# Moving weight sums of a block-form product from VectorE to accumulating transfers, with the late splits moved to the middle of a pair and two more chunks in block form

## The chip, the cores and the metric

The kernel runs on one core of a Trainium2 chip. The metric is the device time of one execution in microseconds. An engine is named as the profile names it: PE is TensorE's matmuls, PEld its weight loads, DVE VectorE, ACT ScalarE, POOL GpSimd, SP SyncE, which here only issues transfers.

## The reference, cut to what matters

One layer over 512 latent tokens (a grid of 8 x 64) of 1024 channels, with 256 context tokens and 16 heads of 64 channels:

```python
h  = rmsnorm(x) * (1 + sc) + sh;  hc = rmsnorm(ctx) * (1 + sc_c) + sh_c
b_gate, c_gate, x_in, z_a, q, k, v, z_b, g_a, g_b = split(h @ w_in)      # 10 parts of 1024 columns
q, k = rope(q), rope(k)                                                 # 2-D rotary
k_c, v_c = split(hc @ w_in[:, K_OFF:V_END])
attn = softmax([q.k over an 8 x 16 window + rpb, q.k_c]) @ [v, v_c]
y_a = (silu(z_a) * b_gate * conv3(c_gate * x_in)) @ w_out_conv
y_b = (silu(z_b) * attn) @ w_out_attn
y   = (sigmoid(g_a) * y_a + sigmoid(g_b) * y_b) @ w_o
out = x + gt * rmsnorm(y)
```

Everything is float32.

## The kernel before

**Products.** A float32 operand is split into a high part H (an ACT cast) and a low part L (a DVE subtraction); the helper `split` does both (L67 the cast, L70 or L73 the subtraction), and a product is three matmuls, H·H, H·L and L·H.

**Chunks.** The weights of the input projection come in chunks of 1 MB, 256 columns each, as two `raw` tiles of 512 KB (4 of 8 row blocks each), loaded by SP (L89). The pool has three `raw` buffers, so the second raw tile of chunk n+1 lies in the buffer of chunk n's first one. In the program's names a chunk is qk (queries and keys of one head pair), v (values), zb (attention's gate), cx and bz (the two chunks of a convolution part) or g (merge gates). `order` lists the chunks in the order in which they are used, and `plan` says which are worked on beside which head pair's attention. A plain chunk is split as it stands and multiplied in 2 x 24 matmuls of 512 columns (L164 to L166). For a chunk that `paired` names, the product is taken in a block form with seven half-size products: `pair` runs 7 x 12 matmuls of 256 columns (L289) into three PSUM banks a, b and e. Its operands of weights are B11, B21, B22 (parts of the raw tiles) and T1 to T4 (sums of parts). `Chunk.first` adds b11+b12 (L102, T1), b11+b22 (L105, T2), b12+b22 (L109, T3) and b21+b11 (L110, T4), in place in the raw tiles, and splits B11, T1, B21 and T2. `Chunk.second` splits T3, T4 and B22 when the pair begins. The qk chunks (`keep`) also need B12, so that their b12+b22 is added in `second`. Twenty chunks are paired before: qk3, 4 and 6, zb0 to zb2, cx5 to 7, bz5 to 7, g0 to g7.

**Attention's slots.** The attention part is 8 head pairs of 8 slots. A slot takes steps of the filling generators (`step(items)`, that is pairs and units of the chunks of this row of `plan`), then the score block two ahead (L717 to L726, softmax on L733 to L747), after every second block the transposes of the weights and their split into TH and TL (L754, then `split`), and once in four blocks the weighted values (`gather`, L773). At a slot's end the functions in `behind` run: there the next chunk's `first` is done. `later` holds functions that are due some steps on: of a paired qk the queries' split and copies (`queries`), and the keys' (`rest`). `rope` rotates one projection with two DVE products and two accumulating transfers on POOL's queue (L626).

**Order.** The instructions of an engine run in the order that the framework's scheduler gives them, apart from those that are held in the order of the program (`keep_in_program_order`). Within a queue each waits for those ahead of it.

The host lays out the weights before the launch; the part b11 of a raw tile is 4 strips of 128 columns of a row of 256.

Of the kernel before, what the change touches and what calls it, by code (L numbers as in the profile page):

```python
# [27 lines left out]
def layer(ctx: ExitStack, tc, xp, ctxt, ctxT, cc, wmod, small, wfirst, win, wout, wo, rel, tab, out):  # L28
# [35 lines left out]
    def split(H, L, src, scale=None, pinned=False):  # L64

        if scale is None:
            cast = nc.scalar.copy(H, src)  # L67
            if pinned:
                tc.keep_in_program_order(cast)
            nc.vector.tensor_sub(L, src, H.bitcast(F32))  # L70
        else:
            nc.scalar.mul(H, src, scale)
# [10 lines left out]
    class Chunk:  # L83
# [7 lines left out]
        def split(self):  # L91
            t = [wtile([P, 4, 2, 256]) for _ in range(2)]
            for x, raw in zip(t, self.raws):
                split(x[:, :, 0], x[:, :, 1], raw)
            k = range(KT)
            return tuple([t[i // 4][:, i % 4, y] for i in k] for y in range(2)) + ([t[i // 4][:, i % 4] for i in k],)

        def first(self, keep=False):
            (b11, b12), (b21, b22) = self.b = [(r[:, :, :P], r[:, :, P:]) for r in self.raws]
            t, sums = (wtile([P, 2, 2, 4, P]) for _ in range(2))  # L100
            split(t[:, 0, 0], t[:, 0, 1], b11)
            nc.vector.tensor_add(b11, b11, b12)  # L102
            split(sums[:, 0, 0], sums[:, 0, 1], b11)
            split(t[:, 1, 0], t[:, 1, 1], b21)
            nc.vector.tensor_add(b11, b11, b22)  # L105
            split(sums[:, 1, 0], sums[:, 1, 1], b11)
            self.keep = keep
            if not keep:
                nc.vector.tensor_add(b12, b12, b22)  # L109
            nc.vector.tensor_add(b21, b21, b11)  # L110
            self.B = {"B11": t[:, 0], "B21": t[:, 1], "T1": sums[:, 0], "T2": sums[:, 1]}
            return self

        def second(self):
            t, last = (wtile([P, 2, 2, 4, P]) for _ in range(2))
            (_, b12), (b21, b22) = self.b
# [11 lines left out]
    class Chunks:  # L128
# [104 lines left out]
    def paired(n, i):  # L233
        return n == "g" or n == "qk" and i in (3, 4, 6) or n == "zb" and i < 3 or n in ("cx", "bz") and i > 4
# [59 lines left out]
    def pair(c1, c2, w=None):  # L294

        w = w or chunk().B
# [3 lines left out]
        nc.scalar.copy(c1[:, first], a)  # L300
        product(b, A12, w["B21"], True)
# [4 lines left out]
        nc.vector.tensor_add(c1[:, first], c1[:, first], b)  # L306
# [324 lines left out]
    def step(items):  # L631
# [4 lines left out]
        next(items)  # L636
        for f, units in due:
# [20 lines left out]
    def keys_queries(p):  # L658
# [35 lines left out]
        if blocks:  # L694
            later.append((queries, 0))
# [508 lines left out]
```

## Time and profile before

| | before |
|---|---|
| median of 3 runs | 709.12 us (709.09 to 709.35) |
| the profiled execution | 709.01 us, of it span 707.2 |
| instructions of PE, DVE, ACT, POOL | 4196, 1114, 868, 110 |
| chunks in block form | 20 |
| transfers of `raw` from the input weights | 74 of 512 KB, 4.4 us to landing |
| accumulating transfers of the rotations (L626) | 32 of 128 KB, 3.6 us to landing |

Times are microseconds from the span's start unless marked ns. A group's row gives its engine, what it writes and reads with partitions x elements, its count, its busy time and the mean of one instruction. In a timeline "[3.08 <-DMA raw<-in_win]" behind a row says that the engine stood idle 3.08 us before it and that this transfer ended the wait. Matmuls overlap, so what one costs is read from the starts of consecutive ones and not from their durations. In the chain of work that ended last, a row is a stretch of one engine's instructions.

### The profile page before, as it was taken

To read this page: it belongs to the slowest core of one execution; us is meant where nothing else is said; L and a number is where in the kernel's file an instruction comes from. 1 tells how busy PE (TensorE), PEld (TensorE's weight loads), DVE (VectorE), ACT (ScalarE), POOL (GpSimd) and SP (SyncE) were. 2 spreads that over 40 slices of the span, in tenths; PEclk is the share of its full clock that TensorE was granted. 3 is DMA by queue.
4 is the path that set the end of the run, shared out by engine and by line. 5 is a ranking of instruction groups with operands and counts; after the bars stand their busy time and mean duration, and the time that the engine had idled before them with its cause. 6 is when DMAs were issued, how large, how long until landed. Compare 5 with 4: busy or idle time off the path is not lost.

```text
span 707.2 us, 11426 instructions
## 1 busy us (share of the span) xinstructions
PE 695.0 (98%) x4196; PEld 618.0 (87%) x4196; DVE 586.3 (83%) x1114; ACT 436.5 (62%) x868; POOL 66.9 (9%) x110
## 2 busy tenths in 40 slices
PE   7999999999999999999999999999999999999996
PEld 4888888888889989898999999999898899988885
DVE  6979997668599989978898797999799676665996
ACT  6566632656577677775876766778693444442563
POOL 0000002230130310301302203000000000000000
PEclk9999999999999999999999999999999999999998
DMA  8996896564351563542635436313733233560013
GB/s 338 406 354 227 284 339 173 131 164 144 99 105 24 135 176 116 127 138 60 168 106 165 103 125 157 101 61 105 247 117 116 87 120 120 198 250 30 31 59 120
DMA packets 37466, 108.27 MB, mean 153 GB/s; under 512 B 5025, under 2 KB 5281, under 8 KB 37410
## 3 DMA queue, kind: packets, MB, share of 16 engines
q1 hardware_dynamic: 28946, 92.20, 37.8%
q0 software_dynamic: 8320, 15.21, 10.7%
q8 instruction: 33, 0.54, 0.3%
q14 instruction: 23, 0.19, 0.1%
q10 hardware_dynamic: 144, 0.13, 0.1%
HBM read 87.07 MB, written 5.24 MB: 131 GB/s over the span
## 4 chain that ended last, share of the span: by engine, by line
PE 91%; DVE 4%; DMA 2%; ACT 1%; issue 1%; SPq 0%; POOL 0%; DVEq 0%; ACTq 0%
PE ps L289 25%; PE ps L164 11%; PE ps L166 11%; PE ps L165 11%; PE ps L177 6%; PE ps L1008 5%; PE ps L773 4%; PE ps L754 3%; PE ps L182 3%; PE ps L717 3%; PE ps L196 2%; PE ps L424 2%; PE ps L428 2%; PE ps L425 2%; DMA fraw<-in_wfirst 1%; PE ps L726 1%
## 5 line engine op out<-in xcount | busy, mean ns | idle before, releaser
L67 ACT CAST w<-raw 128x512 fp32r<-128x512 f32 (+1 forms) x193 | 137.3, 733 | 95.9 <-PE ps L166 31.3
L70 DVE TENSOR_TENSOR w<-raw,w 128x512 fp32r<-128x512 f32 (+1 forms) x193 | 156.6, 824 | 42.3 <-ACT w L67 40.9
L289 PE MATMUL ps<-S,w 128*128 128x256 f32 x960 | 121.9, 283 | 0.0
L289 PEld LDWEIGHTS ps<-S,w 128*128 128x128 f32 x960 | 118.2, 192 | 0.1
L289 PE MATMUL ps<-h,w 128*128 128x256 f32 x720 | 94.0, 284 | 0.6 <-DVE tc L306 0.5
L289 PEld LDWEIGHTS ps<-h,w 128*128 128x128 f32 x720 | 89.9, 191 | 2.5 <-DVE tc L306 0.7
L164 PE MATMUL ps<-h,w 128*128 128x512 f32 x208 | 81.5, 392 | 0.0
L166 PE MATMUL ps<-h,w 128*128 128x512 f32 x208 | 81.2, 390 | 0.0
L165 PE MATMUL ps<-h,w 128*128 128x512 f32 x208 | 81.0, 390 | 0.0
L626 POOL DMA_DIRECT2D tc<-tb x32 | 28.8, 1175 | 286.7 <-DVE tc L624 197.7
L747 ACT ACTIVATE pt<-pt,z 128x512 f32<-128x512 f32 x64 | 43.0, 724 | 6.0 <-DVE z L745 5.9
L166 PEld LDWEIGHTS ps<-h,w 128*128 128x128 f32 x208 | 39.0, 188 | 8.3
L165 PEld LDWEIGHTS ps<-h,w 128*128 128x128 f32 x208 | 39.1, 188 | 8.0
L164 PEld LDWEIGHTS ps<-h,w 128*128 128x128 f32 x208 | 39.1, 188 | 7.9
L67 ACT CAST TH<-ps 128x512 fp32r<-128x512 f32 x64 | 35.8, 589 | 15.5 <-PE ps L754 15.5
L733 DVE CUSTOM_DVE_ANT_1 ps<-ps,bt 128x512 f32<-128x512 f32 x56 | 38.8, 693 | 6.8 <-PE ps L717 6.5
L70 DVE TENSOR_TENSOR TL<-ps,TH 128x512 fp32r<-128x512 f32 x64 | 42.2, 682 | 1.0 <-ACT TH L67 0.7
L754 PE MATMUL ps<-ident,pt 128*128 128x128 f32 x256 | 33.3, 273 | 0.0
L177 PE MATMUL ps<-w,h 128*128 128x512 f32 x128 | 32.3, 394 | 0.0
L754 PEld LDWEIGHTS ps<-ident,pt 128*128 128x128 f32 x256 | 29.2, 140 | 2.1 <-ACT pt L747 0.2
L740 ACT ACTIVATE pt<-ps,m 128x512 f32<-128x512 f32 x32 | 22.0, 688 | 12.5 <-DVE m L733 11.8
L773 PE MATMUL ps<-TH,V 128*128 128x256 f32 (+1 forms) x96 | 28.5, 319 | 0.2 <-ACT TH L67 0.2
(249 smaller groups left out, 1387.8 us busy)
## 6 DMA issues: line engine op xcount, KB each, us to landing
raw<-in_win SPq DMA_DIRECT2D x74, 512.0 KB, 4.4
wm<-in_wmod SPq DMA_DIRECT2D x34, 512.0 KB, 6.4
raw<-in_wout SPq DMA_DIRECT2D x16, 512.0 KB, 3.6
bt<-in_rel SPq DMA_DIRECT2D x16, 256.0 KB, 2.9
tc<-tb POOLq DMA_DIRECT2D x32, 128.0 KB, 3.6
B<-in_wo SPq DMA_DIRECT2D x8, 512.0 KB, 6.4
fraw<-in_wfirst SPq DMA_DIRECT2D x8, 384.0 KB, 8.6
qd<-qd POOLq DMA_DIRECT2D x24, 128.0 KB, 2.3
```

The source lines that it names most:

```text
L67: cast = nc.scalar.copy(H, src)
L70: nc.vector.tensor_sub(L, src, H.bitcast(F32))
L164: nc.tensor.matmul(ps, lhsT=H[k][:, cs], rhs=mH[k], start=k == 0, stop=False)
L165: nc.tensor.matmul(ps, lhsT=H[k][:, cs], rhs=mL[k], start=False, stop=False)
L166: nc.tensor.matmul(ps, lhsT=L[k][:, cs], rhs=mH[k], start=False, stop=k == KT - 1)
L177: nc.tensor.matmul(ps, lhsT=mH[k][:, ts], rhs=both[k].rearrange("p a c -> p (a c)"), start=k == 0, stop=False, skip_group_check=True,)
L289: nc.tensor.matmul(ps, lhsT=w[:, x, k], rhs=act[y][k], start=start and k + o == 0, stop=k == 3 and o == 2, skip_group_check=True,)
L733: nc.vector.tensor_tensor_reduce(out=s3, in0=s3, in1=bt[:, e::4 - e][:, 0:2], scale=-1.0, scalar=3.0e38, op0=ALU.add, op1=ALU.min, accum_o ...
L747: nc.scalar.mul(x, x, z[:, i:i + 1])
L754: nc.tensor.transpose(tp[:, c], pt[:, c * P:(c + 1) * P], ident)
L773: nc.tensor.matmul(o3[:, dst], lhsT=V[p][:, kt, h], rhs=src(t), start=n == 0 and t is TH, stop=n == len(work) - 1 and t is TL,)
L1008: nc.tensor.matmul(out, lhsT=a(x, k, ts), rhs=w[y][k // 2][:, k % 2, cols], start=start and k + o == 0, stop=k == 3 and o == 2, skip_group ...
```

## The change

1. In paired chunks up to zb3 (`late`: the first 34 of `order`), b12+b22 (not for qk) and b21+b11 become accumulating transfers on POOL's queue, 128 x 512 elements each.
2. In these chunks T3 and T4 are split by a new function `third`, which `pair` calls in the middle, after its first four products; the last three products run in the order B22, T3, T4 instead of T4, T3, B22. The outputs' combinations change order.
3. The rotations of a paired qk run at the slot's end, through `behind`. Its queries' split runs in the middle of the next pair (`midway`).
4. Casts of raw tiles (and of T3, T4 and of paired queries) are held in program order.
5. qk7 and zb3 become paired: 22 chunks in block form.
6. The host lays the paired chunks out so that b11, b12, b21 and b22 are each contiguous in a partition.

```diff
         def split(self):
...
-                split(x[:, :, 0], x[:, :, 1], raw)
+                split(x[:, :, 0], x[:, :, 1], raw, pinned=behind is not None)
...
-        def first(self, keep=False):
-            (b11, b12), (b21, b22) = self.b = [(r[:, :, :P], r[:, :, P:]) for r in self.raws]
+        def first(self, keep=False, late=False):
+            (b11, b12), (b21, b22) = self.b = [
+                [x[:, 2 * u:2 * u + 2].rearrange("p k (x c) -> p (k x) c", c=P) for u in range(2)] for x in self.raws
+            ]
+            self.late = late
             t, sums = (wtile([P, 2, 2, 4, P]) for _ in range(2))
-            split(t[:, 0, 0], t[:, 0, 1], b11)
+            split(t[:, 0, 0], t[:, 0, 1], b11, pinned=behind is not None)
             nc.vector.tensor_add(b11, b11, b12)
+            if late and not keep:
+                nc.gpsimd.dma_start(b12, b22, accum_op=ALU.add)
             split(sums[:, 0, 0], sums[:, 0, 1], b11)
-            split(t[:, 1, 0], t[:, 1, 1], b21)
+            split(t[:, 1, 0], t[:, 1, 1], b21, pinned=behind is not None)
             nc.vector.tensor_add(b11, b11, b22)
+            if late:
+                nc.gpsimd.dma_start(b21, b11, accum_op=ALU.add)
             split(sums[:, 1, 0], sums[:, 1, 1], b11)
             self.keep = keep
-            if not keep:
-                nc.vector.tensor_add(b12, b12, b22)
-            nc.vector.tensor_add(b21, b21, b11)
+            if not late:
+                if not keep:
+                    nc.vector.tensor_add(b12, b12, b22)
+                nc.vector.tensor_add(b21, b21, b11)
...
         def second(self):
...
-            for n, x, b in (("T3", t[:, 0], b12), ("T4", t[:, 1], b21), ("B22", last[:, 0], b22)):
-                split(x[:, 0], x[:, 1], b)
+            if not self.late:
+                self.third()
+            split(last[:, 0, 0], last[:, 0, 1], b22)
+
+        def third(self):
+            t = wtile([P, 2, 2, 4, P])
+            (_, b12), (b21, _) = self.b
+            for n, x, b in (("T3", t[:, 0], b12), ("T4", t[:, 1], b21)):
+                split(x[:, 0], x[:, 1], b, pinned=self.late)
                 self.B[n] = x
...
     def paired(n, i):
-        return n == "g" or n == "qk" and i in (3, 4, 6) or n == "zb" and i < 3 or n in ("cx", "bz") and i > 4
+        return n == "g" or n == "qk" and i in (3, 4, 6, 7) or n == "zb" or n in ("cx", "bz") and i > 4
...
         nc.scalar.copy(c1[:, first], a)
+        while midway:
+            midway.pop(0)()
         product(b, A12, w["B21"], True)
         product(e, blocks_h["X1"], w["T1"], True)
         nc.scalar.copy(c2[:, second], e)
         product(a, blocks_h["S2"], w["T2"], False)
         nc.scalar.copy(c2[:, first], a)
         nc.vector.tensor_add(c1[:, first], c1[:, first], b)
+        if c.late:
+            c.third()
         chunk.more()
         yield
-        product(b, A22, w["T4"], True)
+        if c.late:
+            product(e, blocks_h["S4"], w["B22"], False)
+        else:
+            product(b, A22, w["T4"], True)
         product(a, blocks_h["S3"], w["T3"], False)
         nc.scalar.copy(c1[:, second], a)
-        product(e, blocks_h["S4"], w["B22"], False)
-        for cols, x in ((second, c1[:, second]), (first, e)):
+        if c.late:
+            product(b, A22, w["T4"], True)
+        else:
+            product(e, blocks_h["S4"], w["B22"], False)
+        for cols, x in ((first, e), (second, c1[:, second])):
...
-            rope(q, q)
-            rope(k, k)
+            behind.extend([lambda: rope(q, q), lambda: rope(k, k)])
...
-                split(qd[0][:, dst], qe[0][:, dst], q[:, src], 0.125)
+                split(qd[0][:, dst], qe[0][:, dst], q[:, src], 0.125, pinned=blocks)
...
-            later.append((queries, 0))
+            later.append((lambda: midway.append(queries), 0))
```

Lines move down by 1 to 29 in the changed kernel: L289 becomes L304, L70 stays, L626 becomes L654, L67 becomes L66, L717 becomes L746, L754 L783, L773 L802.

DVE around cx5's `first` (raw_2547 and raw_2548 are cx5's raw tiles, w_2575 holds B11 and B21, w_2576 T1 and T2; TL_2343 is the low part of a slot's transposed weights). Before:

```order
L733 ISA ps_2551,m_2554<-ps_2551,bt_1039 128x512
L733 ISA m_2554 128x1
L70 TENSOR_TENSOR w_2575<-raw_2548,w_2575 128x512
L70 TENSOR_TENSOR TL_2343<-ps_2561,TH_2342 128x512
L745 RECIPROCAL z_2470<-z_2470 128x2
L109 TENSOR_TENSOR raw_2547<-raw_2547,raw_2548 128x4x128
L70 TENSOR_TENSOR TL_2343<-ps_2562,TH_2342 128x512
L70 TENSOR_TENSOR w_2576<-raw_2547,w_2576 128x512
L105 TENSOR_TENSOR raw_2547<-raw_2547,raw_2548 128x4x128
L314 SCALAR_TENSOR_TENSOR tc_2483<-tc_2483,tc_2482 128x256
L110 TENSOR_TENSOR raw_2548<-raw_2548,raw_2547 128x4x128
```

and now:

```order
L70 TENSOR_TENSOR TL_2343<-ps_2561,TH_2342 128x512
L70 TENSOR_TENSOR TL_2343<-ps_2562,TH_2342 128x512
L70 TENSOR_TENSOR w_2575<-raw_2547,w_2575 128x512
L342 SCALAR_TENSOR_TENSOR tc_2473<-tc_2473,tc_2472 128x256
L104 TENSOR_TENSOR raw_2547<-raw_2547 128x512
L345 TENSOR_TENSOR tc_2472<-tc_2472,ps_2478 128x256
L762 ISA ps_2661,m_2664<-ps_2661,bt_1039 128x512
L762 ISA m_2664 128x1
L70 TENSOR_TENSOR w_2576<-raw_2547,w_2576 128x512
L70 TENSOR_TENSOR w_2575<-raw_2548,w_2575 128x512
L109 TENSOR_TENSOR raw_2547<-raw_2547,raw_2548 128x512
```

The two sums into b12 and b21 are gone, the split of the second raw tile stands behind both halves of TL instead of ahead of them.

PE in the second half of cx5's pair (ps_2681 to ps_2683 are the banks a, b and e before, ps_2676 to ps_2678 now; w_2673 holds T3 and T4 before and B22 now, w_2674 B22 before, w_2731 T3 and T4 now; S2, S4 and h the activations). Before:

```order
L289 MATMUL ps_2681<-S23_2215,w_2576 128x256 x3
L726 MATMUL ps_2740<-ks_1896,qd_1892 128x256 x2
L726 MATMUL ps_2740<-ks_1896,qe_1894 128x256 x2
L754 MATMUL ps_2752<-ident_73,pt_2469 128x128 x4
L754 MATMUL ps_2753<-ident_73,pt_2556 128x128 x4
L289 MATMUL ps_2682<-h4_86,w_2673 128x256 x3
L289 MATMUL ps_2682<-h5_87,w_2673 128x256 x3
L289 MATMUL ps_2682<-h6_88,w_2673 128x256 x3
L289 MATMUL ps_2682<-h7_89,w_2673 128x256 x3
L289 MATMUL ps_2681<-S20_1617,w_2673 128x256 x3
```

and now:

```order
L304 MATMUL ps_2676<-S23_2215,w_2576 128x256 x3
L783 MATMUL ps_2752<-ident_73,pt_2469 128x128 x2
L783 MATMUL ps_2753<-ident_73,pt_2556 128x128 x4
L304 MATMUL ps_2678<-S40_1620,w_2673 128x256 x2
L304 MATMUL ps_2676<-S20_1617,w_2731 128x256 x2
L304 MATMUL ps_2678<-S40_1620,w_2673 128x256
L304 MATMUL ps_2678<-S41_1739,w_2673 128x256 x3
L304 MATMUL ps_2678<-S42_2073,w_2673 128x256 x3
L304 MATMUL ps_2678<-S43_2218,w_2673 128x256 x3
L304 MATMUL ps_2676<-S20_1617,w_2731 128x256
```

The score block went ahead into the first half, B22's product comes first, and the first two matmuls of T3's stand within it.

POOL's queue around it, each row a transfer, with what it waits for (qd and qe are the queries' halves and ks the keys'). Before:

```order
L683 DMA qd_2434<-qd_2434 64x512 [waits DMASW7_49,DMASW4_49,DMASW3_49]
L683 DMA qe_2436<-qe_2436 64x512 [waits DMASW6_49,DMASW5_49,DMASW0_49]
L690 DMA ks_2439<-ks_2438 64x768 [waits DMASW1_49,Activation_49]
L691 DMA ks_2439<-kl_2440 64x768 [waits DMASW2_49,DVE_49]
L692 DMA ks_2438<-kl_2440 64x768 [waits DMASW1_49]
L626 DMA tc_2866<-tb_3000 64x512 [waits DVE_49]
```

and now:

```order
L712 DMA qd_2434<-qd_2434 64x512 [waits DMASW7_49,DMASW6_49,DMASW2_49]
L712 DMA qe_2436<-qe_2436 64x512 [waits DMASW3_49,DMASW1_49,DMASW0_49]
L106 DMA raw_2547<-raw_2548 128x512 [waits DMAHW5_49,DMAHW7_49,DMASW4_49,DVE_49]
L719 DMA ks_2439<-ks_2438 64x768 [waits DMASW5_49,Activation_49]
L111 DMA raw_2548<-raw_2547 128x512 [waits DVE_49]
L720 DMA ks_2439<-kl_2440 64x768 [waits DVE_49]
L721 DMA ks_2438<-kl_2440 64x768 [waits DMASW5_49]
L111 DMA raw_2737<-raw_2736 128x512 [waits DMASW6_49,DMAHW0_49,DMASW4_49,DMAHW2_49,DVE_49,Activation_49]
L654 DMA tc_2861<-tb_3026 64x512 [waits DMASW2_49,DVE_49]
```

The two sums of cx5 (L106, L111) and the one of qk4 (raw_2736, raw_2737) have come between the copies of queries and keys, and each stands behind the transfers ahead of it.

More of the change, by code (lines that the diff above doesn't have):

```diff
@@ L64, in split @@
     def split(H, L, src, scale=None, pinned=False):
+        cast = nc.scalar.copy(H, src) if scale is None else nc.scalar.mul(H, src, scale)
+        if pinned:
+            tc.keep_in_program_order(cast)
         if scale is None:
-            cast = nc.scalar.copy(H, src)
-            if pinned:
-                tc.keep_in_program_order(cast)
             nc.vector.tensor_sub(L, src, H.bitcast(F32))
         else:
-            nc.scalar.mul(H, src, scale)
             nc.vector.scalar_tensor_tensor(
@@ L114, in second @@
         def second(self):
-            t, last = (wtile([P, 2, 2, 4, P]) for _ in range(2))
-            (_, b12), (b21, b22) = self.b
+            last = wtile([P, 2, 2, 4, P])
+            (_, b12), (_, b22) = self.b
+            self.B["B22"], self.B["B12"] = last[:, 0], last[:, 1]
             if self.keep:
@@ L119, in second @@
                 nc.vector.tensor_add(b12, b12, b22)
-            for n, x, b in (("T3", t[:, 0], b12), ("T4", t[:, 1], b21), ("B22", last[:, 0], b22)):
-                split(x[:, 0], x[:, 1], b)
+            if not self.late:
[6 more added lines that the diff above has]
+                split(x[:, 0], x[:, 1], b, pinned=self.late)
                 self.B[n] = x
-            self.B["B12"] = last[:, 1]
     behind = None
@@ L144, in ready @@
                 c, kind = self.raw.pop(n), self.srcs[n][1]
-                self.ahead[n] = c.first(kind == "qk") if kind else c.split()
+                self.ahead[n] = c.first(kind == "qk", n < 10 + sum(map(len, plan)) + 1) if kind else c.split()
         def __call__(self):
@@ L292, in product, with pair @@
                 )
-    def pair(c1, c2, w=None):
-        w = w or chunk().B
+    midway = []
+    def pair(c1, c2, c=None):
+        c = c or chunk()
+        w = c.B
         a, b, e = (pj()[:, :256] for _ in range(3))
@@ L636, in step @@
         next(items)
+        while midway:
+            midway.pop(0)()
         for f, units in due:
@@ L662, in keys_queries @@
         if blocks:
-            for _ in pair(q, k, w.B):
+            for _ in pair(q, k, w):
                 yield
-            rope(q, q)
-            rope(k, k)
+            behind.extend([lambda: rope(q, q), lambda: rope(k, k)])
         else:
@@ L1147 @@
     win = chunks(ui, order)
+    for n in [*range(10, 16), *(16 + 4 * (p // 2) + p % 2 for p in (3, 4, 6, 7)), *range(19, 32, 4), *range(32, 40)]:
+        win[n] = win[n].reshape(128, 2, 4, 2, 128).transpose(0, 1, 3, 2, 4).reshape(128, 8, 256)
     uo = np.concatenate([units(a["w_out_conv"][0]), units(a["w_out_attn"][0])])
```

## The prediction

> **What bounds the kernel now.** I read the engine totals and the chain first, then a table by stretch, then the timeline of the one stretch that loses time, then the rows that price what the change touches.
>
> ```profile
> PE 695.0 (98%) x4196; PEld 618.0 (87%) x4196; DVE 586.3 (83%) x1114; ACT 436.5 (62%) x868; POOL 66.9 (9%) x110
> ...
> PE 91%; DVE 4%; DMA 2%; ACT 1%; issue 1%; SPq 0%; POOL 0%; DVEq 0%; ACTq 0%
> ```
>
> TensorE works 695.0 of 707.2 us and is 91% of the chain that ended last. Time falls if TensorE gets less to do, or if it waits less; DVE, ACT and transfers matter where they let it run dry. The table by stretch cuts the attention part so that each stretch begins with a new set of weight chunks. Columns: length, then busy time and instructions of PE, PEld, DVE, ACT, POOL, then granted clock, DMA share, GB/s.
>
> ```profile
> core 0: us, PE busy (x) PEld busy (x) DVE busy (x) ACT busy (x) POOL busy (x), PEclk, DMA share, GB/s
> 196.10:236.70 40.60, 40.60 (x274) 37.24 (x273) 39.10 (x92) 32.47 (x77) 6.56 (x11) 1.00 0.34 81
> 236.70:282.90 46.20, 45.02 (x347) 42.81 (x346) 42.28 (x89) 33.75 (x74) 8.24 (x13) 1.00 0.50 142
> 282.90:334.40 51.50, 51.50 (x323) 46.29 (x322) 42.88 (x96) 34.15 (x78) 9.98 (x15) 1.00 0.43 111
> 334.40:378.30 43.90, 43.90 (x346) 42.59 (x345) 39.36 (x81) 33.76 (x73) 6.54 (x11) 1.00 0.51 145
> 378.30:429.80 51.50, 51.50 (x323) 46.29 (x322) 42.70 (x96) 33.91 (x78) 9.99 (x15) 1.00 0.43 111
> 429.80:473.70 43.90, 43.90 (x346) 42.59 (x345) 41.17 (x85) 35.47 (x77) 6.53 (x11) 1.00 0.45 122
> 473.70:512.20 38.50, 38.50 (x276) 36.00 (x275) 34.23 (x68) 28.33 (x56) 0.00 (x0) 1.00 0.48 158
> ```
>
> Every stretch here but one has PE busy for its whole length. The exception is 236.70 to 282.90, which holds the three paired chunks zb0, cx5 and qk4. The stretches at 334.40 (zb1, cx6, qk6) and 429.80 (zb2, cx7, bz7) hold three pairs and 346 matmuls too, and take 43.90 us. With 347 matmuls this one should take 44.0; it takes 46.20, so 2.2 us are lost there. DVE is fullest there, 42.28 us.
>
> ```profile
> 244.39 2.38 SPq L89 DMA_DIRECT2D raw<-in_win  x2
> ...
> 250.24 0.62 ACT L67 CAST w<-raw 128x512 fp32r<-128x512 f32 x1 [3.08 <-DMA raw<-in_win]
> 250.76 0.58 ACT L67 CAST TH<-ps 128x512 fp32r<-128x512 f32 x1
> 250.89 0.69 DVE L70 TENSOR_TENSOR w<-raw,w 128x512 fp32r<-128x512 f32 x1 [2.19 <-ACT w L67]
> ...
> 252.55 0.49 PE L773 MATMUL ps<-TH,V 128*128 128x512 f32 x1 [0.16 <-ACT TH L67]
> ...
> 253.50 0.50 PE L773 MATMUL ps<-TL,V 128*128 128x512 f32 x1 [0.45 <-DVE TL L70]
> ```
>
> How it is lost: cx5's second raw buffer is asked for at 244.39 and lands at about 250.2, 5.8 us later. Its cast stands on ACT ahead of the casts of TH and waits 3.08 us; the DVE half of that split waits 2.19. TH and TL come late, and the weighted-value matmuls of L773, which should follow each other like any 512-column matmul (0.23, below), start 0.95 apart. What is left of the 2.2 follows in the next 18 us, while DVE works off its queue.
>
> **The change, part by part.**
>
> *Two more paired chunks (qk7, zb3).* A plain chunk is 2 x 24 matmuls of 512 columns, a pair 7 x 12 of 256.
>
> ```profile
> 508.61 0.40 PE L164 MATMUL ps<-h,w 128*128 128x512 f32 x1
> ...
> 514.08 0.64 PE L289 MATMUL ps<-h,w 128*128 128x256 f32 x4
> ```
>
> ```profile
> 364.70 0.87 PE ps L754 x8
> 365.58 5.75 PE ps L289 x48
> 371.32 1.88 PE ps L773 x12
> ```
>
> The first pair of rows brackets the second half of zb3's plain chunk: 24 steps from 508.61 to 514.08, 0.228 each, so 48 take 10.94. The chain's row of 48 pair matmuls took 5.75, 0.1198 each, so 84 take 10.06. Saving 0.88 a chunk, **-1.8** for two, all on TensorE's path.
>
> The Trainium skill, "TensorE: Matmul & The Clock Gate", section "Wait — 56ns, not 53.3ns?", says a warm matmul starts every N / 2.4 GHz plus about 2.5 ns; as an estimate from that page 109 and 216 ns, a saving of 1.2 a chunk, 2.4 in all, and a total 0.6 us lower than mine. The trace disagrees at a granted clock of 1.00 (120 and 228 ns), and the sum goes by the trace.
>
> *Sums by accumulating transfer.* Sixteen paired chunks lose DVE additions: twelve lose two (b12+b22, b21+b11), the four qk lose one, 28 in all, each a 256 KB transfer on POOL's queue instead.
>
> ```profile
> 349.22 0.68 DVE L105 TENSOR_TENSOR raw<-raw 128x512 f32<-128x512 f32 x1
> 349.82 0.69 DVE L109 TENSOR_TENSOR raw<-raw 128x512 f32<-128x512 f32 x1
> ...
> 355.07 3.04 PE L289 MATMUL ps<-S,w 128*128 128x256 f32 x24
> ```
>
> ```profile
> raw<-in_win SPq DMA_DIRECT2D x74, 512.0 KB, 4.4
> wm<-in_wmod SPq DMA_DIRECT2D x34, 512.0 KB, 6.4
> raw<-in_wout SPq DMA_DIRECT2D x16, 512.0 KB, 3.6
> bt<-in_rel SPq DMA_DIRECT2D x16, 256.0 KB, 2.9
> tc<-tb POOLq DMA_DIRECT2D x32, 128.0 KB, 3.6
> ```
>
> Additions in a row start 0.60 us apart (349.22, 349.82). In the stretch that stalls five of them leave DVE (zb0 two, cx5 two, qk4 one): 42.28 - 3.0 = 39.3 us of 44.0, what the stretch at 334.40 has (39.36) without losing time. The transfer itself: the nearest row is the rotations' accumulate of half the bytes, 3.6 us to landing, so I bound 256 KB by 3.6 and 7.2, and take 5. It is issued when b11's second sum is done (349.9 for the chunk above); the first half of that pair ends with the 24 matmuls from 355.07, at 357.9. That is 8.0 us, so both ends are hidden, and the sum gets 0 (ends 0 and 0). It costs POOL little: 9% busy, though the rotation's accumulates and the copies of queries and keys now stand in one queue with it.
>
> *Pinned casts, queries mid-pair, rotations at the slot's end.* These move work inside ACT, DVE and POOL without adding any. On DVE the TL splits now stand ahead of cx5's raw splits, so the wait at 250.24 can't hold them up. I take **-1.9** of the 2.2 us; the ends are 0 (the lateness only moves, rival 1) and -2.2. The rotations come up to a slot later, and the queries' copies with them; they are used in the next row of the plan, a stretch of 43.90 away, so 0.
>
> *T3 and T4 split mid-pair.* Before, all three late splits were done as the pair began; now T3 and T4 are cast after the copy that ends the first half, and B22's product stands between.
>
> ```profile
> L70 DVE TENSOR_TENSOR w<-raw,w 128x1024 fp32r<-128x1024 f32 x50 | 60.9, 1221 | 25.3 <-ACT w L67 25.2
> ...
> L306 DVE TENSOR_TENSOR tc<-tc,ps 128x256 f32<-128x256 f32 x12 | 4.9, 412 | 0.0
> ...
> L300 ACT COPY tc<-ps 128x256 f32<-128x256 f32 x12 | 4.5, 378 | 0.8 <-PE ps L289 0.8
> ```
>
> T3's high part is ready after that copy (0.38, the last row) and a cast (0.62), 1.0, and its low part after a subtraction (0.69) more, 1.7, plus DVE's queue. Counted in the new order by the steps above, T3's first product stands 1.9 to 3.8 us behind the end of the first half nearly everywhere, but only 0.9 in cx5, where six transposes and two matmuls lie between. There the high part is 0.1 late, and with one more copy of 0.38 ahead of it on ACT nearly 0.5: I take **+0.4** (ends 0, and 1.0 with the low part late as well).
>
> The same move holds the chunk's first raw buffer, whose T3 half is read last, until mid-pair, and the next chunk's second raw lands in this buffer. From the end of the first half the chain is: copy, cast and subtraction 1.7, landing 4.4, one cast 0.62, and of that split's subtraction what two matmuls don't cover, 0.69 - 0.24: 7.2, and q for DVE's queue. TensorE meanwhile has the second half (36 x 0.1198 = 4.31), the next pair's first product (12, 1.44) and what stands between, such as L773's 1.88: 7.6. Counted place by place in the new order this room is 7.4 (zb3 to g2), 7.6 (bz6 to qk7), 8.0 (g1 to zb3), 8.4, 8.8, 8.9, and over 9.3 elsewhere. With q = 0.4 and landing at 4.4 the shortfall is 0.2; at 4.8, since half the loads come later than the median, 0.6 + 0.4 = **+1.0**. I take the second. The low end is 0 (landing 3.6, as the output weights' loads), the high end is rival 2. The reloads of the convolution's results now queue on SP behind g2's second raw; the product y0 needs them, behind g2 and g3, so 0.
>
> **Sum.** The profiled execution took 709.0 (span 707.2, 1.8 around it); 709.0 - 1.8 - 1.9 + 0.4 + 1.0 = 706.7, and with 0.1 for the median of 709.1: **706.8**. DVE elsewhere: qk7's pair falls into 378.30 to 429.80 and brings some 5.8 us (eight splits and three sums at 0.60, four half-width combinations of 0.41, less two plain splits of 1.22, by the rows above); bz6 takes two sums away: 47.3 of 50.6. Zb3 brings 4.6 to the stretch at 473.70 (a split and a sum fewer), g0 and g1 take 2.4 away: 36.4 of 37.6. Both are tight but not over.
>
> **The rivals.**
>
> 1. *The waits change places, no change.* For it: DVE at 36.4 of 37.6 and 47.3 of 50.6 is nearly as full as 42.28 of 44.0, which stalled; T3's subtraction is now queued on it mid-pair. Against: the fullest undisturbed row, 41.17 of 43.90, loses nothing. If the 1.9 stays lost or turns up again there: 708.7; with the T3 wait of 0.4 at two places more, 709.5.
>
> 2. *The raw buffer comes too late, slower.* Place: the next chunk's second raw. For it: the load at 244.39 took 5.8. If the loads take 5.8 (now beside 256 KB accumulates) and q is 0.7, the chain is 7.2 + 1.4 + 0.7 = 9.3, and the rooms fall short by 1.9, 1.7, 1.3, 0.9, 0.5 and 0.4: 6.7 in place of 1.0, 712.4. It decides for slower from a landing of about 5.5 on, where the shortfalls reach 4.7. Against: 4.4 is the median of 74 loads.
>
> 3. *The accumulating transfers themselves land late, slower.* If they need 9.0 us instead of 5, T3 is late by 1.0 in perhaps half of 16 chunks: +8, 714.8; it decides from about 8.5. Against: 32 accumulates landed in a median of 3.6 with DVE busy 83%. The Trainium skill, "SBUF — State Buffer", section "A bandwidth-pool intuition that's wrong (but worth ruling out)", says a transfer whose descriptors GpSimd writes waits while DVE holds the shared port, some 3100 ns for 620; by that factor of five 3.6 us would be 18, an estimate from the page. The trace has no sign of it in those 3.6 us.
>
> **How the numbers follow.** Forecast 0.60 (its own range 705.2 to 707.7: the 2.2 wholly gone and no raw wait, or the raw wait doubled), rival 1 0.26, rival 2 0.11, rival 3 0.03. This kernel's time can be told from no change at about 0.2%, 1.4 us: under 707.7 is faster, over 710.5 slower. So faster 0.60, same 0.26, slower 0.14. The range takes in rival 1 up to 709.7 and leaves out rivals 2 and 3 and a little below 705.1.
>
> **What would show it.** TensorE has 2 x 84 more half-width matmuls and 2 x 48 fewer wide ones; the stretch of zb0, cx5 and qk4 takes 44.0 to 44.4; the accumulates land under 7.2 us with no ACT wait for them on the chain; ACT's waits for the raw loads in paired chunks sum to more than before. The forecast is wrong if TensorE's idle time between 200 and 520 us is over 3 us, and the releaser named there (raw load, accumulate, or DVE's subtraction) tells which rival.

## The result, and the profile after

The changed kernel takes 719.21 us (median of 4 runs, 718.43 to 720.0), the kernel before 709.11 beside it: a ratio of 1.0141 (95% interval 1.0125 to 1.0157), 10 us slower. The prediction was 706.8 with a range up to 709.7. One execution each of three kernels below took 280 to 1750 us longer than the others of its kernel; the ratios leave them out.

From the page after, the lines that answer to those shown of before:

```profile
PE 699.4 (98%) x4268; PEld 622.9 (87%) x4268; DVE 581.2 (81%) x1113; ACT 440.9 (61%) x887; POOL 91.5 (13%) x138
...
PE 83%; DVE 7%; DMA 5%; ACT 3%; issue 1%; SPq 1%; POOL 0%; DVEq 0%; ACTq 0%
...
raw<-in_win SPq DMA_DIRECT2D x74, 512.0 KB, 4.8
...
raw<-raw POOLq DMA_DIRECT2D x28, 256.0 KB, 3.4
```

TensorE's share of the chain fell from 91% to 83%; what came in is DVE (7%), transfers (5%) and ACT (3%). The 28 accumulating transfers land in 3.4 us, and the raw loads in 4.8 instead of 4.4. DVE is less busy than before (581.2 after 586.3). So the relief of DVE did not shorten the time; TensorE now waits more for the others.

To see where, the span is cut at the same TensorE instructions in both traces (the first context matmul of each qk chunk, the start of zb3, and 800 matmuls before the end). Columns as in the prediction's table; after:

```profile
196.99:239.49 42.50, 41.13 (x276) 37.34 (x274) 36.30 (x88) 31.76 (x76) 8.00 (x13) 1.00 0.41 97
239.49:285.87 46.38, 44.80 (x348) 42.81 (x345) 40.77 (x87) 34.71 (x76) 11.85 (x18) 1.00 0.65 162
285.87:337.42 51.55, 51.55 (x324) 46.19 (x321) 39.99 (x90) 33.03 (x78) 12.89 (x19) 1.00 0.53 132
337.42:381.82 44.40, 44.23 (x348) 42.62 (x346) 38.21 (x80) 33.89 (x75) 9.87 (x15) 1.00 0.62 162
381.82:432.44 50.62, 50.62 (x360) 47.32 (x358) 40.78 (x94) 34.83 (x84) 10.88 (x16) 1.00 0.52 128
432.44:506.05 73.61, 72.39 (x562) 68.97 (x560) 64.91 (x138) 56.80 (x125) 17.00 (x23) 1.00 0.59 143
506.05:533.20 27.15, 24.62 (x197) 23.79 (x194) 22.75 (x42) 21.06 (x42) 1.73 (x2) 1.00 0.69 219
533.20:537.60 4.40, 4.09 (x19) 3.89 (x20) 4.40 (x9) 3.50 (x7) 0.00 (x0) 0.61 0.00 1
537.60:562.20 24.60, 24.58 (x162) 22.36 (x162) 22.97 (x44) 13.24 (x22) 0.00 (x0) 1.00 0.38 127
```

and of before the two rows that matter most (zb0 to qk4; the units up to zb3):

```profile
237.50:283.66 46.16, 44.98 (x348) 42.77 (x346) 42.24 (x89) 33.79 (x74) 8.24 (x13) 1.00 0.51 145
...
430.56:501.20 70.64, 70.64 (x562) 68.56 (x560) 64.63 (x134) 57.35 (x121) 6.21 (x11) 1.00 0.42 121
```

| work | before | after | difference |
|---|---|---|---|
| v1, qk3 | 40.57 | 42.50 | +1.9 |
| zb0, cx5, qk4 | 46.16 | 46.38 | +0.2 |
| v2, bz5, qk5 | 51.49 | 51.55 | +0.1 |
| zb1, cx6, qk6 | 43.92 | 44.40 | +0.5 |
| v3, bz6, qk7 (now a pair) | 51.49 | 50.62 | -0.9 |
| zb2, cx7, bz7, g0, g1 | 70.64 | 73.61 | +3.0 |
| zb3 (now a pair), g2, g3, start of y0 | 51.13 | 56.15 | +5.0 |

From the starts of consecutive matmuls, stalls over 0.1 us add up to 10.5 us between 190 and 720, against 2.0 before. The matmul after a stall also takes 0.1 us more (17 times, 3 before: 1.4 us), and one stretch at half rate costs 1.5 (below). Less the 1.8 of saved work this gives 9.6; the last matmul starts 9.8 later. The stalls lie at four places, but for 0.4 in cx5 (under late T3, below).

*At 207, qk2's keys ahead of TH.* Chain, then ACT's timeline:

```profile
198.34 5.41 DMA tc<-tb
```

```profile
203.84 0.63 ACT L66 CAST ks<-tc 128x512 fp32r<-128x512 f32 x1 [2.97 <-DMA qe<-qe]
...
206.01 0.58 ACT L66 CAST TH<-ps 128x512 fp32r<-128x512 f32 x1
```

The keys' cast needs the rotation's accumulate, the last that landed before it (203.75; qe<-qe, which the row names, landed at 203.93, after the cast's start). It now stands ahead of the second pair of TH casts on ACT, the first of which ran at 202.96 before. TensorE loses 1.9 us at 207 to 209.

*At 249.9 (and 440 to 445), the queries.*

```profile
249.78 0.72 ACT L66 ACTIVATE qd<-tc 128x448 fp32r<-128x448 f32 x2 [2.53 <-DMA tc<-tb]
...
251.23 0.37 ACT L323 COPY tc<-ps 128x256 f32<-128x256 f32 x1 [0.74 <-DVE qe L72]
251.50 0.38 ACT L325 COPY tc<-ps 128x256 f32<-128x256 f32 x1
251.66 1.57 PE L304 MATMUL ps<-S,w 128*128 128x256 f32 x11 [1.49 <-ACT tc L323]
```

ACT stands 2.53 us at qk3's queries' cast, which waits for the rotation's transfers; the copies out of zb0's PSUM banks are behind it, and the matmuls that add to those banks wait for the copies. The old loss at 252 is gone and this took its place: hence +0.2 in that stretch instead of -1.9. Of the 1.5 at 440 to 445 some 0.9 is of this kind (qk7's queries, in zb2's pair).

*At 524 to 537, g2 and g3.* SP's queue, then ACT and TensorE:

```profile
514.10 0.33 SPq L88 DMA_DIRECT2D raw<-in_win  x1
514.48 4.07 SPq L918 DMA_DIRECT2D ur<-usc  x8
518.59 1.99 SPq L920 DMA_DIRECT2D ta<-asc  x2
520.83 0.33 SPq L88 DMA_DIRECT2D raw<-in_win  x1
524.81 0.92 SPq L920 DMA_DIRECT2D tb<-asc  x2
525.82 0.38 SPq L88 DMA_DIRECT2D raw<-in_win  x1
```

```profile
532.59 0.62 ACT L66 CAST w<-raw 128x512 fp32r<-128x512 f32 x1 [1.66 <-DMA raw<-in_win]
...
533.26 0.50 PE L304 MATMUL ps<-h,w 128*128 128x256 f32 x2 [1.78 <-ACT w L66]
```

The reloads into tb wait until zb3's gate has read tb, which in block form comes at the pair's end; g3's second raw is behind them on SP and goes out at 525.82, before at 517.68. TensorE loses 2.5 at 531 to 534, and then runs 15 matmuls at half rate (the row from 533.20: granted clock 0.61). The 1.0 at 524 is another thing: the bank copies of g2 (L323, L325) stand behind casts of the reloaded tiles on ACT, which is busy there without a gap.

*Copies and casts that come a little late* at 369, 453 to 497 and 559: some 1.5 us in pieces of 0.1 to 0.4, behind a bank copy on ACT or a split on DVE where the profile names a releaser.

### The profile page after: what moved, and what is told of

The parts are those of the page before. It is cut to its first block, busy times and chain, and to the rows that moved or that the text cites. A ratio compares the mean times of both kernels' runs of the same rounds, so it can differ in the third digit from the quotient of the medians.

```text
span 717.1 us, 11686 instructions
## 1 busy us (share of the span) xinstructions
PE 699.4 (98%) x4268; PEld 622.9 (87%) x4268; DVE 581.2 (81%) x1113; ACT 440.9 (61%) x887; POOL 91.5 (13%) x138
## 4 chain that ended last, share of the span: by engine, by line
PE 83%; DVE 7%; DMA 5%; ACT 3%; issue 1%; SPq 1%; POOL 0%; DVEq 0%; ACTq 0%
PE ps L304 24%; PE ps L179 10%; PE ps L180 10%; PE ps L181 10%; PE ps L192 6%; PE ps L1037 5%; PE ps L802 3%; PE ps L197 3%; PE ps L783 3%; PE ps L746 2%; DVE w L70 2%; DMA raw<-in_win 2%; DMA tc<-tb 2%; PE ps L452 2%; PE ps L456 2%; PE ps L453 2%
## 5 line engine op out<-in xcount | busy, mean ns | idle before, releaser
L70 DVE TENSOR_TENSOR w<-raw,w 128x512 fp32r<-128x512 f32 (+1 forms) x204 | 160.6, 807 | 47.6 <-ACT w L66 46.8
L66 ACT CAST w<-raw 128x512 fp32r<-128x512 f32 (+1 forms) x204 | 141.0, 718 | 86.5 <-PE ps L181 27.7
L304 PE MATMUL ps<-S,w 128*128 128x256 f32 x1056 | 139.3, 285 | 2.9 <-ACT tc L323 1.5
L304 PEld LDWEIGHTS ps<-S,w 128*128 128x128 f32 x1056 | 132.1, 192 | 6.1 <-ACT tc L323 1.9
L304 PE MATMUL ps<-h,w 128*128 128x256 f32 x792 | 105.9, 286 | 2.2 <-ACT w L66 1.8
L304 PEld LDWEIGHTS ps<-h,w 128*128 128x128 f32 x792 | 100.1, 193 | 4.1 <-ACT w L66 2.0
L179 PE MATMUL ps<-h,w 128*128 128x512 f32 x176 | 68.9, 391 | 0.0
L181 PE MATMUL ps<-h,w 128*128 128x512 f32 x176 | 68.8, 391 | 0.0
L180 PE MATMUL ps<-h,w 128*128 128x512 f32 x176 | 68.6, 390 | 0.0
L654 POOL DMA_DIRECT2D tc<-tb x32 | 28.6, 1192 | 209.2 <-DVE tc L652 183.4
L70 DVE TENSOR_TENSOR TL<-ps,TH 128x512 fp32r<-128x512 f32 x64 | 42.8, 683 | 6.7 <-ACT TH L66 6.7
L66 ACT CAST TH<-ps 128x512 fp32r<-128x512 f32 x64 | 36.0, 585 | 6.1 <-PE ps L783 6.1
L181 PEld LDWEIGHTS ps<-h,w 128*128 128x128 f32 x176 | 33.0, 188 | 7.1 <-DVE w L70 0.2
L179 PEld LDWEIGHTS ps<-h,w 128*128 128x128 f32 x176 | 33.1, 188 | 6.8
L180 PEld LDWEIGHTS ps<-h,w 128*128 128x128 f32 x176 | 33.1, 188 | 6.8
L783 PE MATMUL ps<-ident,pt 128*128 128x128 f32 x256 | 33.3, 272 | 0.0
L783 PEld LDWEIGHTS ps<-ident,pt 128*128 128x128 f32 x256 | 29.3, 140 | 1.9
L802 PE MATMUL ps<-TH,V 128*128 128x256 f32 (+1 forms) x96 | 28.6, 320 | 0.9 <-ACT TH L66 0.9
```

The costliest lines, as they stand in the source:

```text
L66: cast = nc.scalar.copy(H, src) if scale is None else nc.scalar.mul(H, src, scale)
L179: nc.tensor.matmul(ps, lhsT=H[k][:, cs], rhs=mH[k], start=k == 0, stop=False)
L180: nc.tensor.matmul(ps, lhsT=H[k][:, cs], rhs=mL[k], start=False, stop=False)
L181: nc.tensor.matmul(ps, lhsT=L[k][:, cs], rhs=mH[k], start=False, stop=k == KT - 1)
L304: nc.tensor.matmul(ps, lhsT=w[:, x, k], rhs=act[y][k], start=start and k + o == 0, stop=k == 3 and o == 2, skip_group_check=True,)
L783: nc.tensor.transpose(tp[:, c], pt[:, c * P:(c + 1) * P], ident)
```

## The experiments

**Undoing one part of the change.** First the reloads:

```diff
-        nc.sync.dma_start(reloaded[k], usc[k])
+        nc.gpsimd.dma_start(reloaded[k], usc[k])
...
-        nc.sync.dma_start(early[k], asc[k // 2][:, k % 2])
+        nc.gpsimd.dma_start(early[k], asc[k // 2][:, k % 2])
```

> The changed kernel, with one edit: the eight reloads of the convolution's results and the four of the gated attention (ur, ta, tb) are issued on POOL's queue and not on SP's. Theory: they block SP (tb waits for the last instruction of zb3's gate, 3.3 us) and g3's second raw stands behind them, 8 us later than before; TensorE stands 1.9 + 0.4 + 0.2 us at 530 to 534 and then runs 21 matmuls at 0.21 us instead of 0.12 (2.0 us). That goes, the 1.0 at 524 stays: about 719.2 - 4.5 = 714.7. Rival (the accumulating transfers and the late raw buffers are the cause, wherever they show): 718 to 719.5, the wait goes to the next load.

Measured 722.07 (ratio 1.0194, 1.0167 to 1.0221): no gain, but 2.9 us above the changed kernel. What the edit aimed at did come: the reload into tb waits on POOL (8.8 us), no cast waits for g3's second raw, and the stall at 531 and the half rate after it are gone. So the queue on SP was their cause. But other stalls came, first at g2's second raw:

```profile
522.12 0.62 ACT L66 CAST w<-raw 128x512 fp32r<-128x512 f32 x1 [2.33 <-DMA raw<-in_win]
...
522.79 0.50 PE L304 MATMUL ps<-h,w 128*128 128x256 f32 x2 [1.08 <-ACT w L66]
```

That load goes out at 515.99. Counted from the cast before it this is no later than in the changed kernel (514.10, where all runs 1.9 earlier), where no cast waits for it. But it lands after 6.1 us instead of 3.6: the eight reloads now go out on POOL from 512.09 on, ahead of it and beside it, and no longer behind it. Further stalls, of 1.2 at 528 and 1.3 at 540 to 542, come where bank copies stand behind casts of reloaded tiles on ACT. So the edit took away one wait and made others; it says nothing on the held buffer.

The queries and rotations as before (`rope` direct, `later.append((queries, 0))`, no held cast):

> The changed kernel with the queries' split and the rotations where they were before (rotations right behind the pair, queries at the start of the next step, not held in program order). Theory: at 249.9 and at 439.7 to 445 ACT stands 2.5 and 1.6 us at the queries' cast, which waits for the rotations' transfers, with the copies out of the pair's banks behind it; TensorE waits 1.65 and 1.5 for them. That goes: 719.2 - 3.2 = 716.0. Rival: 718.5 to 719.5, since ACT then waits for the same transfers in another place.

Measured 716.66 (1.0106, 1.0091 to 1.0121), 2.5 us under the changed kernel: as expected. The stall at 249.9 is gone. At 440 to 444 there still are 1.5: 0.6 behind an addition on DVE, and 0.9 behind the queries' cast, which waits 1.15 for qk7's rotation in that kernel too.

The raw casts free again (`pinned` taken out of the three splits of raw parts):

> The changed kernel with the casts of the raw tiles not held in program order (those of T3, T4 and of the queries still are). Theory: the held casts made the scheduler put the cast of qk2's rotated keys ahead of those of TH on ACT, where it waits 2.97 us for the rotation's transfer; TensorE lost 1.9 at 207. With the casts free that row stands behind TH again: 719.2 - 1.9 = 717.3. Rival: the wait of before (a raw cast ahead of TH, 2.2 us at 250) comes back in its place: 719 to 720.

Measured 721.11 (1.0169, 1.0153 to 1.0184), above the rival's range too. The stall at 207 is gone, as said, but the time is not, and the rival's wait of 2.2 at 250 is not there either. The largest new stall is 3.0 us at 462; ACT's row, TensorE's, and then the chain:

```profile
465.31 1.66 ACT L66 CAST w<-raw 128x512 fp32r<-128x512 f32 x3 [3.09 <-DMA raw<-in_win]
465.52 0.50 PE L746 MATMUL ps<-ks,qd 128*128 128x512 f32 x1 [2.86 <-DMA ks<-kl]
```

```profile
459.34 6.14 DMA ks<-kl
```

A raw cast does stand ahead of its load on ACT, but the score block waits for something else: the copy of the keys' low half on POOL's queue, whose cast was done by 453.2. It goes out when it did in the changed kernel (459.34, there 459.40) but lands after 6.1 us instead of 2.6. Two raw loads go out at 459.42 and 460.02, there just behind the copy, at 459.92 and 460.52. So neither theory nor rival; that free casts always bring such a wait is not shown. TensorE then runs 11 matmuls at half rate.

The sums on DVE again (`nc.vector.tensor_add` in the places of the two transfers):

> The changed kernel with the 28 sums on DVE again, at the same places in the program, all else as changed. Theory: the accumulating transfers land in 3.4 us and TensorE waits for none of them, and DVE gets 28 x 0.60 = 17 us more work: 719 to 722. Rival (the transfers delay the loads of raw, whose landing went from 4.4 to 4.8 us, and hold the buffers): 712 to 716.

Measured 724.6 (1.0224), 5.4 us above the changed kernel and clear of it, more than expected: within the changed kernel the transfers are a gain. The rival falls.

**Adding one part to the kernel before.** Two more pairs:

> The kernel before with qk7 and zb3 in block form, nothing else of the change (sums on DVE, T3 and T4 split as the pair begins). Theory: the 1.76 us of TensorE are won and more is lost at the places where the changed kernel loses it, qk7's queries and copies at 440 to 445 (1.5) and the reloads behind zb3's gate at 524 to 537 (3 to 5): 711 to 713. Rival (those losses come of the transfers and late splits): 707.6.

Measured 711.75 (1.0037, 1.0024 to 1.0051), in the theory's range, but not at the places that it named: there is no stall at 440 to 445, and at 521 there is one of 1.6, behind an addition on a DVE that is busy without a gap, where 3 to 5 were expected. The others are those of before and 0.6 at 462 and 0.4 at 484.

The raw casts held:

> The kernel before with the casts of raw tiles held in program order, nothing else. Theory: the keys' cast of qk2 goes ahead of TH on ACT, 1.9 us lost at 207, and the 2.2 us at 252 to 271 go or stay: 709.3 to 711.3, with the wait at 207 in the trace. Rival: 707.1, the held casts alone end the lateness at 250.

Measured 713.41 (1.0071, 1.0054 to 1.0087), 2 us above the upper end. The stall at 207 is there (1.8), the one at 252 is not, and there are 0.6 at 251, 0.6 at 479 and 0.3 at 344 and 440.

The sums as transfers, with the splits still as the pair begins:

> The kernel before with only the sums b12+b22 and b21+b11 of the 14 paired chunks in attention's slots as accumulating transfers (and the contiguous layout); T3 and T4 still split as the pair begins, 20 pairs. Theory: that split is due 2 us after the sums are issued, the transfers land in 3.4, so ACT and DVE wait for them with the bank copies and TH behind: 710 to 713. Rival (17 us less on DVE is worth more than the waits): 706.9 to 708.

Measured 712.39 (1.0048, 1.0033 to 1.0063), as expected. The splits do wait for the transfers (ACT 16.1 us in 12 waits, two of them at 463 to 465, where TensorE stalls 1.3). The largest stall, 1.8 at 245, is the queries' though:

```profile
245.98 0.72 ACT L66 ACTIVATE qd<-tc 128x448 fp32r<-128x448 f32 x2 [0.75 <-DMA tc<-tb]
```

The rotation's transfer goes out at 241.08, as early as before (241.42), and lands after 4.8 us instead of 2.9; a bank copy stands behind the cast.

And with T3's and T4's late split:

> As the run before it, and T3 and T4 split in the middle of the pair with B22's product first, as in the changed kernel. Casts of raw free, queries and rotations as before, 20 pairs. Theory: this half of the change is good by itself, the 2.2 us at 252 to 271 go and no wait for a transfer is left: 707.0 to 708.0. Rival (the raw buffer held half a pair longer makes the next second raw late): 710 to 713, with casts waiting for the raw loads in paired chunks.

Measured 712.11 (1.0042, 1.0027 to 1.0057); the expectation of 707 to 708 failed, and this is the central miss. Its largest stall is the queries' again, though queries and rotations are as before:

```profile
248.04 0.72 ACT L66 ACTIVATE qd<-tc 128x448 fp32r<-128x448 f32 x2 [2.83 <-DMA tc<-tb]
...
249.92 1.33 PE L304 MATMUL ps<-S,w 128*128 128x256 f32 x9 [1.66 <-ACT tc L323]
```

Before, at the same cast:

```profile
244.39 0.73 ACT L72 ACTIVATE qd<-tc 128x448 fp32r<-128x448 f32 x2 [0.42 <-DMA tc<-tb]
```

With T4's product last, the queries' half of a qk pair is finished last; the rotation's transfers go out from 242.59 on instead of 240.84, and the second lands at 247.96 instead of 244.34. Half of these 3.6 us is the later start; the other half is a landing of 4.8 us instead of 2.9, as in the run before, where T4's product is not last. What makes it longer no run shows. The rest is a raw load (1.1 us at 271).

Then with the raw casts held too, which is the changed kernel with queries and rotations back and without the two pairs:

> The changed kernel with queries and rotations as before and without the two added pairs: that is the kernel before with accumulated sums, late splits and held raw casts. It stands between the run with the casts free (712.1) and the changed kernel with queries and rotations back (716.7, 22 pairs). Theory: the held casts cost some 2 us (the keys' cast ahead of TH at 207) and the two pairs the rest: 714 to 715. Rival (the two pairs gain their 1.76 here): 718.

Measured 712.98 (1.0045, 1.0029 to 1.0062), under the theory: held casts bring 1.8 + 0.7 at 207 and take away 2.9 at 248 and 271.

And with zb3 in block form on top:

> The changed kernel with queries and rotations as before and qk7 plain, zb3 in block form: between 713.0 (20 pairs) and 716.7 (22). Theory: zb3's pair brings most of the 3.7 us between them, by g3's raw load held on SP behind the reloads (1.9 us of stall, 2 us at half rate): 715.5 to 716.5. Rival (qk7's pair, by its rotations at 440 to 445): 712 to 713.

Measured 716.55 (1.0107, 1.0094 to 1.0120), as expected. That closes a ladder from before to after, each step one part (the first takes in the weights' contiguous layout, which no run tests alone):

| kernel | ratio to before | step, us |
|---|---|---|
| accumulated sums, late splits (712.11) | 1.0042 | +3.0 |
| and raw casts held (712.98) | 1.0045 | +0.2 |
| and zb3 a pair (716.55) | 1.0107 | +4.4 |
| and qk7 a pair (716.66) | 1.0106 | -0.1 |
| and queries, rotations moved: the changed kernel (719.21) | 1.0141 | +2.5 |

(Steps are differences of ratios times 709.1; with intervals of some 0.0015 to each side a step is known to about 1.5 us.)

**Mending it.** The qk chunks left as they were (`late` only where `kind != "qk"`), on accumulated sums and late splits, 20 pairs, casts free:

> Accumulated sums and late splits on the kernel before, 20 pairs, casts free, but not in the qk chunks, whose sums are on DVE and whose splits come as the pair begins, as before. Theory: in the run with all chunks late the queries' half of a qk pair is finished last (T4's product comes last), so the rotation's transfers land 3.6 us later and the queries' cast blocks ACT 2.8 us at 245 to 248, where TensorE loses 1.8; that goes: 712.1 - 1.8 = 710.3, a little less if qk4's late raw at 271 goes too. Rival (contention of the transfers makes the rotation late): 711.5 to 712.5, the wait at 248 stays.

Measured 709.64 (1.0001, 0.9992 to 1.0011): the stall at 248 is gone. So it came of what the change does in the qk chunks; whether of T4's place or of their own accumulating transfers this edit, which takes both away, does not tell. The largest one left is at a held buffer:

```profile
454.00 0.93 SPq L88 DMA_DIRECT2D raw<-in_win  x2
...
460.50 1.14 ACT L66 CAST w<-raw 128x512 fp32r<-128x512 f32 x2 [3.07 <-DMA raw<-in_win]
...
462.32 0.95 PE L304 MATMUL ps<-h,w 128*128 128x256 f32 x6 [1.64 <-DVE tc L345]
```

Both loads go out as cx7's late splits end, one behind the other, and the first lands after 6.5 us. Ten such pairs of loads go out in this trace between 190 and 560, where the kernel before has two; their first lands in a median of 4.3 us and their second in 5.1, a single load in 4.4. So going out in pairs alone does not explain the 6.5.

The queries a step later instead (`later.append((queries, 1))`), with all chunks late:

> Accumulated sums and late splits on the kernel before, 20 pairs, casts free, and the queries' split of a paired qk one step later (behind the next half pair instead of ahead of it). Theory: the cast of the queries no longer stands ahead of the bank copies on ACT: no stall at 248, 712.1 - 1.8 = 710.3. Rival: the queries' copies come too late for the next head pair's scores, 712 to 714, with a wait at L747 or L756 for qd or qe.

Measured 711.89 (1.0039, 1.0026 to 1.0052): neither side. The stall at 248 shrank from 1.8 to 1.3 only: in the trace the queries' cast (247.65, after a wait of 2.25) still stands ahead of the bank copies on ACT, so the edit did not move it past them.

Both edits:

> The two edits together (qk chunks early, queries a step later), on accumulated sums and late splits with 20 pairs. Theory: no wait for rotations left, only those for the raw loads of the late chunks (some 0.5 to 1): 708.0 to 709.5, that is, level with the kernel before or a little under it. Rival (something else takes the place): 711 to 713.

Measured 709.58 (1.0004, 0.9994 to 1.0015), at the upper end of the theory.

T3 split early on a DVE sum, only b21+b11 as a transfer (11 of them):

> The run with both edits (qk chunks early, queries a step later, 20 pairs), but b12+b22 on DVE and T3 split as the pair begins in all chunks, as before; only b21+b11 is an accumulating transfer and only T4 is split mid-pair (12 transfers). Theory: the raw buffer that the next chunk's second raw needs is free as early as before and its load no longer starts together with the one after it (454.0: both issued 0.6 apart, landing after 6.4 us, ACT blocked 3.1 us at 460); DVE still loses 12 sums: 707.5 to 708.5. Rival (DVE needs all 24 sums gone, or the place of the wait changes again): 709.0 to 711.

Measured 713.87 (1.0071, 1.0054 to 1.0088); wrong by 6 us, and worth it. The transfer b21 += b11 reads b11 in the first raw tile, so this buffer is not free when T3 is split but when the transfer has landed:

```profile
255.17 0.91 POOL L109 DMA_DIRECT2D raw<-raw  x1 [3.62 <-DVE tc L342]
...
263.37 0.62 ACT L66 CAST w<-raw 128x512 fp32r<-128x512 f32 x1 [3.03 <-DMA raw<-in_win]
...
264.31 1.94 PE L304 MATMUL ps<-S,w 128*128 128x256 f32 x14 [1.39 <-ACT tc L323]
```

The transfer issued at 255.17 lands at 258.49, 3.3 us later, and the load of qk4's second raw goes out at 258.55; its cast then stands ahead of the bank copies on ACT. The same comes again at 452: the transfer lands at 452.08, the load goes out at 452.14, its cast waits 2.97 us, and TensorE loses 1.2.

The same with zb3 as a pair, not late, and the reloads into ta and tb on POOL:

> The run before it with zb3 in block form (not late), and the reloads into ta and tb issued on POOL's queue, so that they don't hold g3's raw on SP. Theory: 0.88 us of TensorE won, no stall at 520 to 537: 0.5 to 1 us under the run before it, 706.7 to 708. Rival (g2's and g3's raws are late anyway, since ACT and DVE are full with the reloads' splits there): 1 to 3 us above it.

Measured 714.05 (1.0070), level with the run before it. No stall is left after 494: with zb3's splits early and the reloads into ta and tb on POOL the place at 520 to 537 is clean. What each of the two brings no run tells. The 0.88 us of TensorE went to new stalls elsewhere (1.1 at 437).

Accumulated sums and late splits in zb0 and cx5 alone, where DVE was full:

> The kernel before (20 pairs, casts free, queries and rotations as before), with accumulated sums and late splits in zb0 and cx5 alone, the two chunks of the stretch that loses 2.2 us before (4 transfers). Theory: DVE is relieved where it is full and no other buffer is held: 707.0 to 708.0, with no stall over 0.2 us between 240 and 275. Rival (the held buffer or a cast ahead of TH brings the loss back in that stretch): 709 to 711.

Measured 707.96 (0.9986, 0.9977 to 0.9996), as expected, and the one version that beats both kernels, by little: the interval ends just short of no change, and it is the best of 17 versions. Its only wait of TensorE after 190 (0.47 by the starts, at 269, over the 0.2 that was allowed), and the cast that stood 3.08 us before:

```profile
PE ps L304 <- DVE tc L345: 0.3, 1, 0.3
```

```profile
252.77 1.66 ACT L66 CAST w<-raw 128x512 fp32r<-128x512 f32 x3 [1.19 <-DMA raw<-in_win]
```

That cast now stands behind TH's on ACT (248.51), so its wait holds up nothing, though its load goes out later than before (248.31, before 244.39). DVE is busy 40.6 us in the 46.2 from 236.70 on, before 42.28. Which of the two, the order or the relief, brought the gain is not shown.

Last, the run with both edits and cx7 early:

> The run with both edits (qk chunks early, queries a step later, 20 pairs; 709.6) with cx7 early as well, so that the buffer that bz7's second raw lands in is free in time. Theory: the stall at 460 goes (0.4 to 1.8 us, it differs from execution to execution): 708.0 to 709.0. Rival: 709.5 to 711, the wait shows at another late chunk.

Measured 709.45 (1.0002, 0.9993 to 1.0012): above the theory, at the rival's lower end. Freeing this buffer brought no gain clear of noise; where the kernel stalls is open.

## Why the prediction was wrong, point by point

- *TensorE's work, -1.8*: right in size. The stretch with qk7 fell from 51.49 to 50.62, by 0.87.
- *"The reloads now queue on SP behind g2's second raw; the product y0 needs them, so 0"*: the largest miss. I asked who needs the reloads, not who is queued behind them: g3's raw. SP waits for tb until 524.81, the raw comes late, and TensorE loses 2.5 and then runs at half rate; with the reloads off SP (e1) that wait is gone. Making zb3 a pair, forecast as 0.9 won, cost 4.4 (e9 to e15); the 1.0 at 524 and the late T3, which delays g2's second raw and with it the reloads, are in that, and their shares are open.
- *The 2.2 us of waits, -1.9*: the old wait did go, with DVE at 40.8 instead of 42.2. The step "the rotations come up to a slot later, and the queries' copies with them; they are used in the next row of the plan, so 0" failed. I priced when the result is used, not what stands behind the waiting cast on ACT: the bank copies of the running pair. It cost 2.5 us by e2. A second form of it, a rotation that lands late in the qk chunks, cost about as much by e8 and e10, and e7 shows it too; its cause is open.
- *Held casts, 0*: they cost 1.9 at 207, and without them as much is lost elsewhere (e9 against e8; e3, by another wait); in e6 alone they cost 4. Not a term that can be had from one side.
- *Accumulating transfers hidden, 0 and 0*: in the changed kernel TensorE and ACT wait for none, and they landed in 3.4, under my low bound of 3.6. What was left out is that they read the first raw tile and hold it some 3.4 us (e13).
- *Late T3, +0.4, and the raw buffer, +1.0*: right in kind. In cx5 T3's high part is 0.25 late, at 266 (0.12 at 263 waits for a bank copy). At the held buffers single stalls are 1.1 (e8, 271) and 1.8 (e10, 460), where the loads took 5.2 and 6.5 us. That is rival 2's mechanism, at two places and not at six.
- *DVE elsewhere*: the forecast of 47.3 us in the stretch with qk7 was too high by far; it measured 40.8 of 50.6. So the tightness that rival 1 built on was not there.
- *The rivals*: rival 3 did not occur. Rivals 1 and 2 both occurred in part. The sign that was named did show: TensorE was idle 4.3 us between 200 and 520 (busy 315.66 of 320.00), over 3. But the releasers there are mostly ACT's copies and casts, none of the three listed. No rival had a transfer's wait that stops an in-order queue with unrelated work behind it, and three of those (207, 249.9, 531) make most of the 10 us.

## What to carry to other kernels

When a step is moved in time, go through each queue that it passes and ask what stands behind it there until its inputs arrive, not only who needs its result: here ACT stood 2.5 to 3.0 us and SP over 3 us at an instruction that waited, with bank copies, TH's casts and a weight load behind it. An accumulating transfer in place of an addition held its source as long as its landing, some 3.4 us against 0.6. Used in two chunks of the fullest stretch it came with a gain of 0.14%, used in all late chunks it came with a loss. In a kernel that is 98% TensorE, no step of the ladder was a gain clear of noise. And when an edit does not bring what it should, look whether the wait that it aimed at is still there: in e1 it was gone, and the edit had made others.

## What the runs showed of the hardware

A stall of about 2 us can cost more than its length. After the 1.9 us stall at 531 TensorE ran from 533.2 to 537.6 at a granted clock of 0.61, its 256-column matmuls 0.214 apart instead of 0.120, 1.5 us more. It does not always happen: after the 1.65 us at 249.9, and after 2.4 us at 252 in e4, the next matmuls were at full rate but for one or two; after 2.3 at 207 in e15 and 3.0 at 462 in e3, 10 and 11 were slow. The length of the stall alone does not decide it: at 207, 1.9 and then 0.7 us in e1 had no slow matmul behind them, 1.5 and then 0.7 in e4 had eleven or so. In all five traces that have a stretch at clock 0.50 ahead of the kernel's end (after, e3, e4, e9, e15) it lasts 3.4 us. The Trainium skill, "TensorE: Matmul & The Clock Gate", section "What's actually happening", puts the fall to half rate at an idle window of about 3.4 us; here stalls shorter than that were enough at times, with smaller ones near them.

A small copy takes about twice as long beside a weight load. In the trace of before, the copies of queries and keys on POOL's queue (L682 to L692, 190 to 500) land in a median of 2.5 us, 43 of them, but in 5.4 where a 512 KB load of raw is in flight as the copy goes out, 11 of them; in the changed kernel in 2.6 (46) and 4.8 (8). The accumulating transfers show no such split over the traces taken together: the 256 KB ones land in 3.4 either way (23 beside a load, 276 not), the rotations' in 3.5 (62) and 3.6 (359). Why the two kinds differ no run shows.
